# Expert outputs of the first layer written by scatter in token order and read back by plain loads

## The chip, the cores and the metric

One core of a Trainium2 chip runs the whole program in one launch. The core has a matrix engine (PE, with its weight loads as PEld), a vector engine (DVE), a scalar engine (ACT), a general engine (POOL) and a queue engine (SP). Each takes its instructions in order and waits on semaphores. Transfers between SBUF and DRAM run on 16 DMA engines and are issued from SP, ACT or POOL; such an issue stands in the engine's instruction order like any other. The metric is device time in microseconds (us) of one execution, lower is better.

## What is computed

A two-layer transformer over 256 image tokens and 256 context tokens, width 1024, all in 32 bits. Only the first layer updates the context, so its expert part works on 512 tokens (4 tiles of 128). What matters here is the expert part:

```python
def moe_ffn(h, ...):                       # h: tokens x 1024
    scores = sigmoid(t @ w_router)         # 16 experts in 4 groups of 4
    # best group, then its two best experts; their scores, normalised, are the gates
    for e in range(16):
        hid = silu(t @ w_gate[e]) * (t @ w_up[e])      # 1024 -> 256
        out = out + gates[:, e:e+1] * (hid @ w_down[e])  # 256 -> 1024
x = x + g2 * moe_ffn(...)                  # g2: a row of 1024, from the modulation
hx = rms_norm(x, norm1_g) * (1 + sc1) + sh1            # next layer's input
px = hx @ w_in                                          # next layer's projections
```

## The kernel before

Every product of the first layer runs as three 32-bit-reduced products (`mm3`): each operand is split into a high part (ACT casts, `whi`, `Xh`) and the rest (DVE subtracts, `wlo`, `Xl`).

**Experts of the first layer (`experts`, from L1006).** A token goes to two experts. For each of the 16 experts a list of at most 128 token numbers (`idx`) is made by the router. An indirect DMA from POOL gathers those rows of `h2row` (DRAM) into `xg` (L1025); PE transposes them, multiplies by gate and up (`first`), then by down (`second`, into two `y` banks of PSUM). ACT copies the banks to a `y` tile (L211; three such tiles take turns) and writes its 128 rows to `yrows` in DRAM from its own queue (`write`, L1095). So `yrows` is in order of expert and slot. The loop is software-pipelined: expert n's gate and up products stand beside the down products of expert n-1, and `write` comes one step later again. The second half of each w_down is split on POOL instead of DVE (L235 with engine POOL).

**From the first layer to the second (`next_in`, from L760).** `combine` fetches for each of the 4 token tiles the two rows of each token from `yrows` with two indirect DMAs on POOL (8 in all, L1393), by the row numbers `rows` that the router worked out. `sum_pairs` then has four steps a tile: `one` (ACT, L1405) scales the first by its gate, `both` (DVE, L1408) adds the second times its gate, `times` (L1411) multiplies by g2 (DVE for tile 0, POOL for tiles 1 to 3), `add` (DVE, L1414) adds to x. `tokens_in` normalises x: `square` (ACT, L226), `ms` (DVE, L219), `rstd` (a power on POOL, L221), `scale` (DVE `xn`, L655), `turn` (8 PE transposes, `tp`), `modulate` (`xf`, 4 columns blocks on ACT, 4 on DVE L684), `high` (ACT `Xh`), `low` (DVE `Xl`, L694). PE then runs 24 products of the first block of w_in for the tile. The order of these steps on each engine is written out by hand in `next_in`. The first w_in halves are split by four ACT casts and four DVE subtracts first (`parts`); the whi tiles of this stage lie where tiles of the expert stage lay, and so wait for their last readers.

**Waits.** The framework adds semaphore waits from overlaps of what instructions read and write. A scatter into a DRAM tensor counts as writing all of it.

Of the kernel before, what the change touches and what calls it, by code (L numbers as in the profile page):

```python
# [23 lines left out]
D = 1024  # L24
# [53 lines left out]
def shape_constants():  # L78
# [17 lines left out]
    k[:, C_GW:C_GW + 4] = np.array([4, 3, 2, 1], np.float32)  # L96
    k[:, C_TOK:C_TOK + 8] = np.tile(np.arange(4)[None, :] * 128 + i - NONE, 2)
    k[:, C_MH:C_EXP] = -0.5
# [76 lines left out]
class Model:  # L175
# [70 lines left out]
    def run(self, over):  # L246
        tc, nc, a = self.tc, self.nc, self.a
        self.over = over
        with ExitStack() as ctx:
# [8 lines left out]
            self.h2row = self.dram.tile([512, D], F32, name="h2row")  # L258
            self.yrows = self.dram.tile([NEXP * SLOTS * max(self.npass), D], F32, name="yrows")
            self.prow = self.dram.tile([PROWS, D], F32, name="prow")  # L260
# [264 lines left out]
    def layer(self, l):  # L525
# [51 lines left out]
        if paired:  # L577
            with self.psums(PS_PAIR):
                self.expert_pairs(l, mo, route)
        else:  # L580
            with self.psums(PS_MOE):
                self.experts(l, mo, route[0])
                self.gates, self.rows = route[1:]
        self.ring.close(mo)
# [175 lines left out]
    def next_in(self, l):  # L760

        ps = {}
        with self.tc.tile_pool(name="cb", bufs=1, side="right", reuse_waits="tile") as cb, self.tc.manual_schedule():
# [220 lines left out]
    def out_proj(self, l, work, mods):  # L984

        nc = self.nc
        route = Route(self, l, work, mods)
        fw = spread(FILL[l][2], 8)
        for cb in range(2):
            cs = slice(cb * 512, cb * 512 + 512)  # L990
            for t, ps in self.units("w_out", l, cb, [[t] for t in self.qtiles], self.mix_h, self.mix_l, self.q0,
                                    self.parts("w_out", l, cb)):
                if (t, cb) == (self.q0, 0):

                    route.modulation()
# [8 lines left out]
        return route.lists(), route.gates, route.rows  # L1004

    def experts(self, l, mo, lists):  # L1006
# [12 lines left out]
        def gather(n):  # L1019
# [3 lines left out]
            if n < 3:  # L1023
                nc.gpsimd.memset(xg[n], 0.0)
            nc.gpsimd.indirect_dma_start(  # L1025
                out=xg[n % 3], out_offset=None, in_=self.h2row[:, :],
                in_offset=bass.IndirectOffsetOnAxis(ap=lists[ps][:, e:e + 1], axis=0),
                bounds_check=T * 128 - 1, oob_is_err=False)
# [60 lines left out]
        def write(n):  # L1089
            ps, e = order[n]  # L1090
            y = mo.tile([128, D], F32, tag="y", name="y", bufs=3)
            for hf in range(2):
                self.copy(y[:, hf * 512:hf * 512 + 512], ys[n][hf], True)
            r0 = (e * self.npass[l] + ps) * SLOTS
            self.written = nc.scalar.dma_start(self.yrows[r0:r0 + SLOTS, :], y)  # L1095

        ring.until(l)
        with self.tc.manual_schedule():
# [6 lines left out]
            for n in range(N + 1):  # L1105
                if n:
                    turn(n - 1)
                if n > 1:
                    write(n - 2)
# [13 lines left out]
                if n == N - 1:  # L1123
                    ring.load(n=1)
            write(N - 1)

# [259 lines left out]
    def combine(self, l, cb):  # L1386

        self.pairs_of = {}
        n = NEXP * SLOTS * self.npass[l]
        for i, t in enumerate((0, 1, 2, 3) if l == 0 else (2, 3)):  # L1390
# [265 lines left out]
class Route:  # L1656


    def __init__(self, m, l, work, mods):
# [16 lines left out]
        self.gates = m.rt.tile([128, 2, T], F32, tag="gates", name="gates")  # L1676
        self.rows = m.rt.tile([128, 2, T], I32, tag="rows", name="rows")
        self.oh = tile_("oh", [2, T, 16])
        self.pos = tile_("pos", [2, T])
# [43 lines left out]
    def choose(self, x, i, r):  # L1723
# [92 lines left out]

        V.tensor_scalar(self.val[:, :, i], self.oh[:, :, i], cst[:, C_TOK + i:C_TOK + i + 1], None, OP.mult)
        self.picked(self.ips, i)
# [21 lines left out]
    def lists(self):  # L1840

        m, V, T = self.m, self.nc.vector, self.T
        lists, first = [], self.work.tile([128, 2, T], F32, name="first")
        for ps in range(m.npass[self.l]):
            ips = self.ips
            if ps == 0:
                V.tensor_copy(first, self.pos)
            else:
# [4 lines left out]
            idx = m.rt.tile([128, 16], I32, tag=f"idx{ps}", name="idx")  # L1853
# [5 lines left out]
        pick, e = self.small([2, T, 16], "picke"), self.small([2, T], "e")  # L1859
        V.tensor_tensor(pick, self.oh, self.k["cst"][:, C_EXP:C_EXP + 16].unsqueeze(1).unsqueeze(1).broadcast_to(  # L1860
            [128, 2, T, 16]), OP.mult)
        V.reduce_sum(e, pick, axis=AX.X)
        V.scalar_tensor_tensor(self.rows, e, float(SLOTS * m.npass[self.l]), first, OP.mult, OP.add)

# [42 lines left out]
    def extra(self):  # L1907
# [8 lines left out]
        V.tensor_scalar(eid, eid, 15.0, float(16 * self.l), OP.min, OP.add)  # L1916
        idf = small(1, "idf")
        V.scalar_tensor_tensor(idf, eid, 128.0, cst[:, C_ROW:C_ROW + 1], OP.mult, OP.add)
# [92 lines left out]
```

## Time and profile before

| | |
|---|---|
| time, median of 3 runs (lowest to highest) | 888.96 us (886.82 to 890.14) |
| the profiled execution's own time | 888.22 us |
| its span, first to last instruction | 886.3 us |
| PE busy over the span | 784.3 us (88%) |
| DVE, ACT, POOL busy | 582.4, 447.6, 222.2 us |
| experts of the first layer | about 336 to 501 us |
| first layer's experts to second layer's first products | about 500 to 546 us |

The span is that of one profiled execution; times on the trace count from its start. The profiled execution's time is 1.9 us above its span. Whatever delays PE at the border between the layers delays all that follows.

### The profile page before, as it was taken

What the parts mean: (1) busy time and instruction counts of PE and PEld (TensorE: products, weight loads), DVE (VectorE), ACT (ScalarE), POOL (GpSimd) and SP (SyncE); (2) the same over time, 40 slices, a digit from 0 to 9 for tenths busy, and PEclk for the clock granted to TensorE, in tenths of its full rate; (3) what the DMA queues carried; (4) which work ended last, traced back from release to release, by engine and by line L of the source; (5) the groups of instructions that cost most, each with busy time, mean ns of one, the idle gap of its engine ahead of it and who ended that gap; (6) DMA issues with size and microseconds to landing.
All of it is one profiled execution on the core that took longest, in us unless ns stands there. A gap on an engine that the chain in (4) does not pass through costs nothing.

```text
span 886.3 us, 12972 instructions
## 1 busy us (share of the span) xinstructions
PE 784.3 (88%) x4731; PEld 576.3 (65%) x4731; DVE 582.4 (66%) x1200; ACT 447.6 (50%) x861; POOL 222.2 (25%) x258
## 2 busy tenths in 40 slices
PE   4899999889989977999999549998899797999984
PEld 0578878445557746999999438887555565656541
DVE  1577673879863798899999586697667566221226
ACT  2454442667773416888888546462466543111112
POOL 2000101556320133443342472100423101000200
PEclk9999999999999988999999859999899997999987
DMA  9952221667879337899993757342188955999981
GB/s 319 344 185 96 95 96 48 247 270 284 275 214 376 121 148 263 306 388 401 400 408 156 249 195 292 128 158 95 51 331 215 340 186 215 350 423 422 419 333 51
DMA packets 54505, 219.18 MB, mean 247 GB/s; under 512 B 10299, under 2 KB 10299, under 8 KB 36640
## 3 DMA queue, kind: packets, MB, share of 16 engines
q1 hardware_dynamic: 40816, 182.34, 55.0%
q0 software_dynamic: 8736, 24.92, 7.9%
q10 hardware_dynamic: 4880, 11.00, 3.2%
q8 instruction: 39, 0.64, 0.3%
q14 instruction: 34, 0.28, 0.1%
HBM read 207.09 MB, written 16.84 MB: 253 GB/s over the span
## 4 chain that ended last, share of the span: by engine, by line
PE 66%; DVE 16%; DMA 8%; ACT 3%; issue 3%; POOL 2%; SPq 0%; ACTq 0%; POOLq 0%; DVEq 0%
PE mm L207 7%; PE mm L206 7%; PE mm L205 7%; PE tp L193 6%; PE gu L1189 6%; PE ada L459 4%; PE gu L207 4%; PE gu L205 3%; PE gu L206 3%; DMA wraw<-in_w_up 3%; PE sc L1466 3%; PE w L1245 3%; DVE wlo L235 2%; PE w L1154 2%; DVE nm L1480 2%
## 5 line engine op out<-in xcount | busy, mean ns | idle before, releaser
L235 DVE TENSOR_TENSOR wlo<-wraw,whi 128x1024 fp32r<-128x1024 f32 x136 | 186.1, 1392 | 43.0 <-ACT whi L234 40.5
L234 ACT CAST whi<-wraw 128x1024 fp32r<-128x1024 f32 x152 | 152.8, 1050 | 57.7 <-PE mm L207 35.5
L205 PE MATMUL mm<-whi,Xh 128*128 128x512 f32 x288 | 116.3, 405 | 5.1 <-ACT Xh L690 4.7
L206 PE MATMUL mm<-wlo,Xh 128*128 128x512 f32 x288 | 115.3, 400 | 0.5 <-DVE wlo L235 0.5
L207 PE MATMUL mm<-whi,Xl 128*128 128x512 f32 x288 | 115.0, 399 | 0.5 <-DVE Xl L694 0.5
L221 POOL TENSOR_TENSOR rstd<-ms,cst 128x1 f32<-128x1 f32 (+2 forms) x34 | 29.4, 864 | 272.1 <-DVE ms L219 263.2
L1493 ACT ACTIVATE e<-sc,nm 128x512 f32<-128x512 f32 (+1 forms) x96 | 58.4, 613 | 42.4 <-DVE nm L1486 22.6
L207 PE MATMUL gu<-whi,xl 128*128 128x256 f32 x256 | 74.3, 290 | 0.0
L205 PE MATMUL gu<-whi,xh 128*128 128x256 f32 x256 | 74.2, 290 | 0.0
L206 PE MATMUL gu<-wlo,xh 128*128 128x256 f32 x256 | 72.7, 284 | 0.0
L1189 PE MATMUL gu<-wraw,xq 128*64 128x256 f32 x512 | 64.4, 396 | 3.7 <-DMA wraw<-in_w_up 3.7
L205 PEld LDWEIGHTS mm<-whi,Xh 128*128 128x128 f32 x288 | 55.1, 191 | 18.7 <-ACT Xh L690 6.2
L207 PEld LDWEIGHTS mm<-whi,Xl 128*128 128x128 f32 x288 | 55.0, 191 | 13.9 <-DVE Xl L694 1.5
L206 PEld LDWEIGHTS mm<-wlo,Xh 128*128 128x128 f32 x288 | 55.1, 191 | 12.8 <-DVE wlo L235 1.2
L235 POOL TENSOR_TENSOR wlo<-wraw,whi 128x1024 fp32r<-128x1024 f32 x16 | 42.7, 2672 | 81.1 <-ACT whi L234 50.3
L1189 PEld LDWEIGHTS gu<-wraw,xq 128*64 128x64 f32 x512 | 37.9, 142 | 24.1 <-DMA wraw<-in_w_up 4.2
L193 PEld LDWEIGHTS tp<-ident,e 128*128 128x128 f32 x240 | 26.1, 142 | 40.8 <-issue 21.1
L1480 DVE TENSOR_REDUCE nm<-sc 128x1 f32<-128x512 f32 x64 | 41.2, 684 | 16.5 <-PE sc L1466 11.6
L207 PEld LDWEIGHTS gu<-whi,xl 128*128 128x128 f32 x256 | 49.3, 193 | 1.1 <-DVE xl L1050 0.4
L205 PEld LDWEIGHTS gu<-whi,xh 128*128 128x128 f32 x256 | 49.6, 194 | 0.3 <-ACT xh L1049 0.3
L206 PEld LDWEIGHTS gu<-wlo,xh 128*128 128x128 f32 x256 | 49.5, 193 | 0.0
L193 PE MATMUL tp<-ident,e 128*128 128x128 f32 x240 | 37.8, 286 | 8.4 <-DVE e L1534 3.9
(348 smaller groups left out, 1625.4 us busy)
## 6 DMA issues: line engine op xcount, KB each, us to landing
wraw<-in_w_ada SPq DMA_DIRECT2D x40, 1024.0 KB, 4.9
wraw<-in_w_gate SPq DMA_DIRECT2D x32, 1024.0 KB, 10.1
wraw<-in_w_up SPq DMA_DIRECT2D x32, 1024.0 KB, 11.0
wraw<-in_w_down SPq DMA_DIRECT2D x32, 1024.0 KB, 14.1
wraw<-in_w_in SPq DMA_DIRECT2D x14, 1024.0 KB, 5.2
wraw<-in_w_ada SPq DMA_DIRECT2D x16, 512.0 KB, 8.1
yrows<-y ACTq DMA_DIRECT2D x16, 512.0 KB, 8.1
wraw<-in_w_in POOLq DMA_DIRECT2D x5, 1024.0 KB, 11.9
```

The source lines that it names most:

```text
L193: self.nc.tensor.transpose(out, in_, self.k["ident"][:n, :n])
L205: mm(out, lhsT=xh, rhs=wh, start=start, stop=False)
L206: mm(out, lhsT=xh, rhs=wl, start=False, stop=False)
L207: mm(out, lhsT=xl, rhs=wh, start=False, stop=stop)
L221: nc.gpsimd.tensor_tensor(r, ms, self.k["mhalf"][:, :width], OP.pow)
L234: nc.scalar.copy(h, raw[:, lo:hi])
L235: (engine or nc.vector).tensor_tensor(l, raw[:, lo:hi], h.bitcast(F32), OP.subtract)
L459: nc.tensor.matmul(ps[32 * j:32 * j + 32, :], lhsT=self.silu_c[:, kc, :], rhs=raw[:, 512 * j:512 * j + 512], start=kc == 0, stop=kc == NKC ...
L1189: nc.tensor.matmul(gu[PSLOTS * g:PSLOTS * g + PSLOTS, 256 * b:256 * b + 256], lhsT=xq[q][:, kc, c:c + PSLOTS], rhs=raw[:, kc * 256:kc * 25 ...
L1245: nc.tensor.matmul(y[hf][gs], lhsT=hT[:, c, 0:PSLOTS] if p == NP else hT[:, c, gs], rhs=raw[:, c * D + o * 512:c * D + o * 512 + 512], sta ...
L1480: V.reduce_max(self.nm[:, i:i + 1], self.ps[i], axis=AX.X)
L1493: nc.scalar.activation(self.e[i][:, :self.nkey], self.ps[i], AF.Exp, scale=0.125, bias=self.nm[:, i:i + 1], accum_out=self.z[i])
```

## The change

Each expert's output rows are now scattered by an indirect DMA from POOL (new L1094) into `orow`, a DRAM tensor of 1024 rows in which token t's two results are rows 2t and 2t+1; empty slots get a row number out of bounds and are skipped. `combine` no longer gathers: for each tile two plain DMAs of 512 KB load the rows 2t (from SP's queue) and 2t+1 (from ACT's). The router makes one list `outs` of row numbers from the same one-hot product as before, and gets the token list `idx` from it by a shift; the old `rows` are not worked out any more. The g2 products of all four tiles run on DVE, and the hand-written order of `next_in` is changed. At the end of `experts`, the output of expert 14 is copied and written right after its products.

```diff
-    k[:, C_TOK:C_TOK + 8] = np.tile(np.arange(4)[None, :] * 128 + i - NONE, 2)
+    k[:, C_TOK:C_TOK + 8] = 2 * (np.arange(8)[None, :] // 2 * 128 + i) + np.arange(8)[None, :] % 2 - 2 * NONE
...
-            for name, t in (("one", 0), ("both", 0), ("times", 0), ("one", 1), ("add", 0)):
+            for name, t in (("one", 0), ("one", 1), ("both", 0), ("times", 0), ("add", 0)):
                 step(sums, t, name)
             step(ins, 0, "square")
             step(sums, 1, "both")
             step(ins, 0, "root")
-            step(sums, 1, "times", self.nc.gpsimd)
             step(sums, 2, "one")
             for t in range(1, 6):
                 step(ins, t - 1, "scale")
-                step(sums, t + 1, "both")
-                step(sums, t + 1, "times", self.nc.gpsimd)
-                step(sums, t, "add")
+                step(sums, t, "times")
                 for h in range(2):
                     step(ins, t - 1, "turn", h)
                     step(ins, t - 1, "modulate", h)
                 half(t - 2, 1)
                 step(ins, t - 1, "high", 0)
                 step(ins, t - 1, "high", 1)
+                step(sums, t, "add")
                 step(ins, t, "square")
                 step(sums, t + 2, "one")
                 step(ins, t - 1, "low", 0)
                 step(ins, t, "root")
+                step(ins, t - 1, "low", 1)
+                step(sums, t + 1, "both")
                 if t == 1:
                     self.ring.until(2, self.nc.gpsimd)
-                step(ins, t - 1, "low", 1)
                 half(t - 1, 0)
...
-            r0 = (e * self.npass[l] + ps) * SLOTS
-            self.written = nc.scalar.dma_start(self.yrows[r0:r0 + SLOTS, :], y)
+            self.written = nc.gpsimd.indirect_dma_start(
+                out=self.orow[:, :], out_offset=bass.IndirectOffsetOnAxis(ap=lists[ps][1][:, e:e + 1], axis=0),
+                in_=y, in_offset=None, bounds_check=2 * T * 128 - 1, oob_is_err=False)
...
-                if n > 1:
+                if 1 < n < N:
                     write(n - 2)
...
                 if n == N - 1:
                     ring.load(n=1)
+                    write(n - 1)
             write(N - 1)
...
-            y = [cb.tile([128, D], F32, tag="yc", name="yc", bufs=8) for _ in range(2)]
+            y = cb.tile([128, 2, D], F32, tag="yc", name="yc", bufs=4)
             for w in range(2):
-                self.nc.gpsimd.indirect_dma_start(
-                    out=y[w], out_offset=None, in_=self.yrows[:n, :],
-                    in_offset=bass.IndirectOffsetOnAxis(ap=self.rows[:, w, i:i + 1], axis=0),
-                    bounds_check=n - 1, oob_is_err=False)
-            self.pairs_of[t] = y, i
+                (self.nc.scalar if w else self.nc.sync).dma_start(y[:, w], rows[i, :, w])
+            self.pairs_of[t] = [y[:, w] for w in range(2)], i
...
-            V.tensor_scalar(idx, ips[:, 0:16], float(NONE), None, OP.add)
-            lists.append(idx)
+            V.tensor_scalar(out, ips[:, 0:16], 2.0 * NONE, None, OP.add)
+            V.tensor_single_scalar(idx, out, 1, OP.logical_shift_right)
+            lists.append((idx, out))
```

The scalar engine's order at the end of the expert loop and the start of `next_in` (the last row of casts splits the first w_in block) was before:

```order
L1067 ACTIVATE hid<-gu 128x256
L1077 CAST hh<-hT 128x256
L211 COPY y<-y 128x512 x2
L1095 DMA yrows<-y 128x1024
L211 COPY y<-y 128x512 x2
L1095 DMA yrows<-y 128x1024
L156 DMA wraw<-in_w_in 128x4x512
L234 CAST whi<-wraw 128x1024 x4
L1405 ACTIVATE yc<-yc,gates 128x1024 x2
```

and the same place on the same engine is now:

```order
L234 CAST whi<-wraw 128x1024 x3
L156 DMA wraw<-in_w_in 128x4x512
L234 CAST whi<-wraw 128x1024
L1067 ACTIVATE hid<-gu 128x256
L211 COPY y<-y 128x512 x2
L1077 CAST hh<-hT 128x256
L211 COPY y<-y 128x512 x2
L234 CAST whi<-wraw 128x1024 x4
L1396 DMA yc<-orow 128x1024 x4
L1405 ACTIVATE yc<-yc,gates 128x1024 x2
```

The writes have left this engine, the w_in load stands earlier, and the four loads of the second results stand behind the four casts. On POOL, from the split of the last w_down halves to the normalisation of the second layer's input, stood before:

```order
L235 TENSOR_TENSOR wlo<-wraw,whi 128x1024 x5
L1393 DMA yc<-yrows,rows 128x1024 x8
L221 TENSOR_TENSOR rstd<-ms,cst 128x1
L1411 TENSOR_TENSOR yc<-yc,wraw 128x1024 x2
L221 TENSOR_TENSOR rstd<-ms,cst 128x1
```

and now there stands, one scatter behind each split and the last two together:

```order
L235 TENSOR_TENSOR wlo<-wraw,whi 128x1024
L1094 DMA orow<-y,outs 1024x1024
L235 TENSOR_TENSOR wlo<-wraw,whi 128x1024 x2
L1094 DMA orow<-y,outs 1024x1024 x2
L221 TENSOR_TENSOR rstd<-ms,cst 128x1 x2
L156 DMA wraw<-in_w_in 128x4x512 x5
```

The eight gathers and the products are gone from POOL and sixteen scatters have come. In the built program each scatter waits for the landing of the scatter before it. On DVE the steps between one tile's scaling (`xn`) and the next tile's were before:

```order
L655 TENSOR_SCALAR xn<-xc,rstd 128x1024
L1408 SCALAR_TENSOR_TENSOR yc<-yc,gates 128x1024
L1414 TENSOR_TENSOR x_109<-x_109,yc 128x1024
L684 TENSOR_SCALAR xf<-tp,sc_2522,sh_2521 128x128 x4
L694 TENSOR_TENSOR Xl<-xf,Xh 128x4x128
L219 TENSOR_SCALAR ms<-nss 128x1
L694 TENSOR_TENSOR Xl<-xf,Xh 128x4x128
L655 TENSOR_SCALAR xn<-x_109,rstd 128x1024
```

and are now, for the same tile:

```order
L656 TENSOR_SCALAR xn<-xc,rstd 128x1024
L1411 TENSOR_TENSOR yc<-yc,wraw 128x1024
L685 TENSOR_SCALAR xf<-tp,sc_2522,sh_2521 128x128 x4
L1414 TENSOR_TENSOR x_109<-x_109,yc 128x1024
L695 TENSOR_TENSOR Xl<-xf,Xh 128x4x128
L219 TENSOR_SCALAR ms<-nss 128x1
L695 TENSOR_TENSOR Xl<-xf,Xh 128x4x128
L1408 SCALAR_TENSOR_TENSOR yc<-yc,gates 128x1024
L656 TENSOR_SCALAR xn<-x_109,rstd 128x1024
```

A product has come in, the sum to x has moved behind `xf`, and `both` of the tile after next has moved from the front to just ahead of the next `xn`.

## Rows read from the trace of the kernel before

**Rows 1.** Windows: length, PE, PEld, DVE, ACT, POOL busy (count), PEclk, DMA share, GB/s.

```profile
400.00:450.00 50.00, 50.00 (x363) 46.81 (x362) 47.71 (x47) 44.30 (x63) 21.08 (x10) 1.00 1.01 401
505.00:518.00 13.00, 0.00 (x0) 0.00 (x0) 10.19 (x10) 7.48 (x9) 10.34 (x10) 0.50 0.92 312
526.00:546.00 20.00, 20.00 (x89) 16.45 (x89) 13.22 (x25) 9.99 (x23) 9.22 (x9) 0.86 0.87 320
```

**Rows 2.** Timeline of PE, 518 to 546 us: the four tiles' transposes.

```profile
520.51 1.97 PE L193 MATMUL tp<-ident,xn 128*128 128x128 f32 x8 [20.12 <-DVE xn L655]
...
530.04 1.87 PE L193 MATMUL tp<-ident,xn 128*128 128x128 f32 x8
...
537.22 1.03 PE L193 MATMUL tp<-ident,xn 128*128 128x128 f32 x8
...
543.62 1.09 PE L193 MATMUL tp<-ident,xn 128*128 128x128 f32 x8
```

**Rows 3.** The chain that ended last, 500 to 504 us: start, us, what.

```profile
500.44 0.59 ACT y L211
501.05 2.96 DMA yrows<-y
```

**Rows 4.** Timeline of POOL, 490 to 518 us.

```profile
491.53 5.99 POOL L235 TENSOR_TENSOR wlo<-wraw,whi 128x1024 fp32r<-128x1024 f32 x2 [7.09 <-ACT whi L234]
504.95 1.00 POOL L1393 DMA_INDIRECT yc<-yrows,rows  x1 [7.43 <-DMA yrows<-y]
...
517.57 2.33 POOL L1411 TENSOR_TENSOR yc<-yc,wraw 128x1024 f32<-128x1024 f32 x1
```

**Rows 5.** Timeline of DVE, 511 to 535 us.

```profile
511.76 1.28 DVE L1408 SCALAR_TENSOR_TENSOR yc<-yc,gates 128x1024 f32<-128x1024 f32 x1 [0.79 <-DMA yc<-yrows,rows]
513.08 1.23 DVE L1411 TENSOR_TENSOR yc<-yc,wraw 128x1024 f32<-128x1024 f32 x1
514.34 1.23 DVE L1414 TENSOR_TENSOR xc<-xc,yc 128x1024 f32<-128x1024 f32 x1
...
516.78 0.15 DVE L219 TENSOR_SCALAR ms<-nss 128x1 f32<-128x1 f32 x1
517.62 2.83 DVE L655 TENSOR_SCALAR xn<-xc,rstd 128x1024 f32<-128x1024 f32 x1 [0.69 <-POOL rstd L221]
...
527.00 0.75 DVE L655 TENSOR_SCALAR xn<-xc,rstd 128x1024 f32<-128x1024 f32 x1 [0.45 <-POOL rstd L221]
...
531.95 1.37 DVE L684 TENSOR_SCALAR xf<-tp,sc,sh 128x128 f32<-128x128 f32 x4 [1.86 <-PE tp L193]
533.33 0.76 DVE L694 TENSOR_TENSOR Xl<-xf,Xh 128x512 fp32r<-128x512 f32 x1
```

**Rows 6.** Timeline of ACT, 490 to 512 us.

```profile
504.11 1.99 ACT L234 CAST whi<-wraw 128x1024 fp32r<-128x1024 f32 x2 [3.08 <-DMA yrows<-y]
```

**Rows 7.** The eight gathers into yc, issue to landing.

```profile
DMA to landing us min/median/max: 4.3/5.5/6.2
```

**Rows 8.** Timeline of POOL, 452 to 463 us, inside the expert loop.

```profile
452.58 2.65 POOL L235 TENSOR_TENSOR wlo<-wraw,whi 128x1024 fp32r<-128x1024 f32 x1 [5.13 <-issue]
455.61 1.57 POOL L1025 DMA_INDIRECT xg<-h2row,idx  x1 [0.39 <-ACT xh L1049]
462.33 2.63 POOL L235 TENSOR_TENSOR wlo<-wraw,whi 128x1024 fp32r<-128x1024 f32 x1 [5.15 <-ACT whi L234]
```

**Rows 9.** The gathers into xg, 395 to 450 us, issue to landing.

```profile
DMA to landing us min/median/max: 9.2/9.5/10.0
```

**Rows 10.** The writes of y, 395 to 450 us, issue to landing.

```profile
DMA to landing us min/median/max: 7.9/8.1/8.4
```

**Rows 11.** Timelines of DVE, POOL and PE at the router's end, 334 to 342 us.

```profile
334.74 0.17 DVE L1854 TENSOR_SCALAR idx<-ips 128x16 int32<-128x16 f32 x1
...
335.75 1.14 POOL L1025 DMA_INDIRECT xg<-h2row,idx  x1 [5.99 <-DVE gates L1867]
...
340.17 1.55 PE L193 MATMUL tp<-ident,xg 128*128 128x128 f32 x8 [2.00 <-DMA xg<-h2row,idx]
```

More of the change, by code (lines that the diff above doesn't have):

```diff
@@ L258, in run @@
             self.h2row = self.dram.tile([512, D], F32, name="h2row")
-            self.yrows = self.dram.tile([NEXP * SLOTS * max(self.npass), D], F32, name="yrows")
+            self.orow = self.dram.tile([1024, D], F32, name="orow")
             self.prow = self.dram.tile([PROWS, D], F32, name="prow")
@@ L582, in layer @@
                 self.experts(l, mo, route[0])
-                self.gates, self.rows = route[1:]
+                self.gates = route[1]
         self.ring.close(mo)
@@ L1003, in out_proj @@
             return route
-        return route.lists(), route.gates, route.rows
+        return route.lists(), route.gates
     def experts(self, l, mo, lists):
@@ L1026, in gather @@
                 out=xg[n % 3], out_offset=None, in_=self.h2row[:, :],
-                in_offset=bass.IndirectOffsetOnAxis(ap=lists[ps][:, e:e + 1], axis=0),
+                in_offset=bass.IndirectOffsetOnAxis(ap=lists[ps][0][:, e:e + 1], axis=0),
                 bounds_check=T * 128 - 1, oob_is_err=False)
@@ L1388, in combine @@
         self.pairs_of = {}
-        n = NEXP * SLOTS * self.npass[l]
-        for i, t in enumerate((0, 1, 2, 3) if l == 0 else (2, 3)):
-            y = [cb.tile([128, D], F32, tag="yc", name="yc", bufs=8) for _ in range(2)]
+        tiles = (0, 1, 2, 3) if l == 0 else (2, 3)
+        rows = self.orow[:, :].rearrange("(i p w) d -> i p w d", p=128, w=2)
+        for i, t in enumerate(tiles):
+            y = cb.tile([128, 2, D], F32, tag="yc", name="yc", bufs=4)
             for w in range(2):
-                self.nc.gpsimd.indirect_dma_start(
-                    out=y[w], out_offset=None, in_=self.yrows[:n, :],
-                    in_offset=bass.IndirectOffsetOnAxis(ap=self.rows[:, w, i:i + 1], axis=0),
-                    bounds_check=n - 1, oob_is_err=False)
-            self.pairs_of[t] = y, i
+                (self.nc.scalar if w else self.nc.sync).dma_start(y[:, w], rows[i, :, w])
+            self.pairs_of[t] = [y[:, w] for w in range(2)], i
     def sum_pairs(self, t):
@@ L1676, in __init__ @@
         self.gates = m.rt.tile([128, 2, T], F32, tag="gates", name="gates")
-        self.rows = m.rt.tile([128, 2, T], I32, tag="rows", name="rows")
-        self.oh = tile_("oh", [2, T, 16])
+        self.oh = tile_("oh", [2, T, 16], F16)
         self.pos = tile_("pos", [2, T])
@@ L1815, in choose @@
                                    accum_out=self.pos[:, w, i:i + 1])
-        V.tensor_scalar(self.val[:, :, i], self.oh[:, :, i], cst[:, C_TOK + i:C_TOK + i + 1], None, OP.mult)
+        V.tensor_tensor(self.val[:, :, i], self.oh[:, :, i], cst[:, C_TOK + 2 * i:C_TOK + 2 * i + 2].unsqueeze(2)
+                        .broadcast_to([128, 2, 16]), OP.mult)
         self.picked(self.ips, i)
@@ L1842, in lists @@
         m, V, T = self.m, self.nc.vector, self.T
-        lists, first = [], self.work.tile([128, 2, T], F32, name="first")
+        lists = []
         for ps in range(m.npass[self.l]):
             ips = self.ips
-            if ps == 0:
-                V.tensor_copy(first, self.pos)
-            else:
+            if ps:
                 V.tensor_scalar(self.pos, self.pos, -float(SLOTS), None, OP.add)
@@ L1852, in lists @@
                     self.picked(ips, i)
-            idx = m.rt.tile([128, 16], I32, tag=f"idx{ps}", name="idx")
-            V.tensor_scalar(idx, ips[:, 0:16], float(NONE), None, OP.add)
-            lists.append(idx)
+            idx, out = (m.rt.tile([128, 16], I32, tag=f"{n}{ps}", name=n) for n in ("idx", "outs"))
+            V.tensor_scalar(out, ips[:, 0:16], 2.0 * NONE, None, OP.add)
+            V.tensor_single_scalar(idx, out, 1, OP.logical_shift_right)
+            lists.append((idx, out))
         if m.over is not None:
             V.reduce_max(m.over[:, self.l:self.l + 1], self.pps[:, 64:80], axis=AX.X)
[L1859 to L1863, printed above, removed]
         pick, gsum, g = self.small([2, T, 16], "pickg"), self.small([T], "gsum"), self.gates
@@ L1916, in extra @@
         V.tensor_scalar(eid, eid, 15.0, float(16 * self.l), OP.min, OP.add)
-        idf = small(1, "idf")
+        idf = small(1, "px")
         V.scalar_tensor_tensor(idf, eid, 128.0, cst[:, C_ROW:C_ROW + 1], OP.mult, OP.add)
```

## The prediction

> **What bounds the kernel now.** I read the busy time by stretch first, since shares over the whole span mix stages. In the expert loop PE is busy for all of 50.00 us at full clock [rows 1]; a change of what surrounds it there costs or gives nothing until PE has to wait. At the border between the layers it is the other way round: from 505 to 518 us PE does nothing. So the second view is PE's timeline there [rows 2]: its first transposes start at 520.51 after 20.12 us of idle time that DVE's `xn` ended; the next three tiles' transposes follow at 530.04, 537.22 and 543.62 with PE busy all the way (20.00 of 20.00 us) [rows 1]. The first gap is at half the granted clock and PE keeps it for some 10 us after it starts again. What lies in the gap I take from the chain that ended last and the timelines of the other engines. The last y tile is copied by 501.03, its write lands 2.96 us after issue, at 504.0 [rows 3]; POOL's first gather starts at 504.95 [rows 4]; the second row of tile 0 has landed at 511.76, when DVE's `both` starts [rows 5]; from there it is a chain of `both`, `times`, `add`, square, root, `xn` to PE. Three things are to be seen. ACT's first w_in cast waited 3.08 us for the last write of y, since its tile takes the place of y [rows 6]. DVE's first `xn` took 2.83 us, the second 0.75 us: the first ran beside POOL's `times`, which began at 517.57 [rows 4, 5]. And eight gathers by POOL are what the tiles wait for, at 4.3 to 6.2 us from issue to landing [rows 7].
>
> **The expert loop: sixteen writes move from ACT to POOL.** ACT loses an issue per expert; PE is the bound there, so that gives nothing. POOL gets one indirect DMA per expert. The nearest row is its own gather there, 1.57 us; the scatter comes when the y copies are done, and POOL sits idle 5.15 us before its next `wlo` [rows 8]: the issue is hidden, 0. If that cover went, the second half of w_down would come late and PE would wait for it. One rule speaks against the move: the gather of 1.57 us ran beside DVE's subtracts, others without them took 1.0 us, as the first of [rows 4]. The Trainium skill (SBUF — State Buffer, Who interferes with whom) says that a DMA issued from POOL can be starved of descriptors by DVE and that one issued from ACT or SP cannot; the trace agrees with a stretch of 0.6 us and no more, which fits in the idle time, so that by row and rule alike the sum gets 0.
>
> The scatters carry a wait that the writes did not have: each waits for the landing of the one before. Behind the waiting one on POOL stand the next `wlo` and gather. In the loop a scatter is due every 9.75 us (462.33 - 452.58 [rows 8]); gathers land after 9.2 to 10.0 us there [rows 9], writes of y after 7.9 to 8.1 and 8.4 [rows 10]. I take 8 to 9, below the period, as the loop loses the ACT queue's 512 KB per expert and gets only the filled slots back: 0. The other end is a rival below.
>
> **The border, term by term.** POOL's last split ended at 497.5 [rows 4], and scatter 14 stands behind it. ACT's load of w_in needs the slot that POOL's split before reads, and now stands ahead of the cast for the last split: I let that make the split end some 0.3 later, and start scatter 14 at 498.0. Scatter 15 needs its copy (501.0) and the landing of scatter 14. No row shows a scatter in an idle stretch. Bounds: 2.96 us, the last plain write [rows 3], and 6.2 us, the slowest gather [rows 7]; I take 4.3 us, the fastest gather, which is issued by the same engine in the same way with empty queues. Then scatter 14 lands at 502.3, scatter 15 starts at 502.7 (0.4 us from a landing to the next issue, less than the 0.95 us of the gather that followed the write [rows 3, 4], as it waits for less) and lands at 507.0. The four casts, behind the same y tiles' release, take 4.0 us (1.99 for two [rows 6]) to 511.1, as w_in has long landed. Only behind them does ACT issue its loads: 511.4. A load of 512 KB lands after 2.96 us alone [rows 3] or 5.5 us amid the others [rows 7]; SP's four loads are still under way, so 4.0 us: tile 0 is complete at 515.4, against 511.76 before, +3.6 us.
>
> DVE's `xn` for tile 0 now runs without POOL's product beside it: 0.75 in place of 2.83 us, -2.1 us [rows 5].
>
> Then the tile loop. DVE's work between two `xn` is now 0.75 + 1.23 (`times`) + 1.37 (`xf`) + 1.23 (`add`) + two `Xl` of 0.76 + 0.15 (`ms`) + 1.28 (`both`) = 7.5 us [rows 5]. PE's period at full clock is 543.62 - 537.22 = 6.4 us [rows 2]. While PE is at half clock (530.04 - 520.51 = 9.5 us) DVE's 7.5 us are hidden; for the two periods after that they are not, 2 x 1.1 = +2.2 us. Lower bound +1.0 (DVE's instructions overlap by some 0.08 us each, eight of them, twice); upper bound +3.4, if `ms`, which stands ahead of the second `Xl`, also makes DVE wait 0.6 us for ACT's square, now that `add` comes later.
>
> At the router `idx` comes some 0.3 us later: `outs` takes its place, of 0.17 us, and a reduce stands between the two [rows 11]. POOL's first gather follows `idx`, and PE's first transposes waited 2.00 us for that gather [rows 11]: +0.3 us. `picke`, `e` and `rows` fall away behind it, hidden: 0. Putting expert 14's copies ahead of `hh` costs 0: the copies and `hh` both had to be done before the last products.
>
> Sum: 3.6 - 2.1 + 2.2 + 0.3 = +4.0 us. From 526 us PE runs without a gap [rows 1], so the delay goes through to the end. On the profiled execution's 888.22 us that is 892.2; the median of the runs is 0.7 higher, so I say 893.0 for the median.
>
> **Rivals.** What a measurement of this kernel can tell from no change is about 0.5%, 4.4 us: 884.5 to 893.4.
>
> *Writes that land fast.* If the scatters land in 2.96 us, as the last plain write did [rows 3]: scatter 14 at 501.0, scatter 15 from 501.4 to 504.4, casts to 508.4, ACT's loads at 508.7, tile 0 at 512.5 with the same 4.0 us, +0.7 - 2.1 + 2.2 + 0.3 = +1.1: 890. For it: a write needs no read of DRAM ahead. Against it: issue by POOL alone takes 1 us. The Trainium skill (DMA: Bandwidth & Descriptors, Anatomy of one DMA) puts a POOL-issued transfer at 2.0 us plus bytes at 436 GB/s, an estimate of 2.6 us for the half-filled 512 KB; by that the sum would be about 0.7 us lower than this rival's.
>
> *Slower: the chain of scatters falls behind in the loop.* They share POOL's software queue with the gathers, which land after 9.2 to 10.0 us [rows 9]. From a landing of 9.75 us on each scatter is later than the one before. At 10.3 us it is 0.56 us per expert over some 11 experts at full DMA load, 6 us; I let 2 us of that be hidden, half in POOL's idle time [rows 8] and half between a split and its products, and PE waits some 4 us: 897. The same sign has a landing of 6.2 us twice at the border: +3.8, 897 too.
>
> *Faster.* If the writes land fast and DVE's longer loop is hidden behind PE after all: 0.7 - 2.1 + 0.3 = -1.1, 888; less than 884.5 needs ACT's loads to land without the wait for the casts too, 4 us earlier. Nothing in the order of ACT lets that happen.
>
> **Chances.** Sum as worked out (892 to 894.5): 0.53, of which 0.31 under 893.4. Writes that land fast: 0.20. Late scatters: 0.23. Faster: 0.04. So faster 0.04, same 0.31 + 0.20 = 0.51, slower 0.22 + 0.23 = 0.45. The likeliest is 893.0, by itself 891 to 895. The range goes from 889 (the fast landing with the lower bound of the loop) to 898 (the late scatters).
>
> **What would show it.** The scatter of expert 15 starting some 0.4 us after the landing of that of expert 14; the first w_in cast near 507; ACT's yc loads issued near 511 and tile 0's `both` near 515.4; `xn` at 0.75 us; PE's first transposes near 522 and the third and fourth 7 to 8 us apart. In the loop PE stays at 100% and POOL's `wlo` starts as soon as ACT's cast is done. I am wrong if scatters land in under 3 us or over 6 us at the border, if PE has gaps in the loop, or if PE's transposes stay 6.4 us apart.

## The result and the profile after

The changed kernel took 896.18 us (median of 4 runs, 895.66 to 899.16) beside 888.8 us for the kernel before (4 runs, 886.82 to 890.14): a ratio of 1.0093, 95% interval 1.0066 to 1.0119. By the medians it is 7.4 us slower; the ratio stands for 8.3 us (5.9 to 10.6). The profiled execution took 899.16 us with a span of 897.3 us, 3 us above the median, so positions on its trace stand up to 3 us later than in a usual run. I compare distances between landmarks, not positions.

Windows of the profile after, with the columns of [rows 1]:

```profile
400.00:450.00 50.00, 49.46 (x357) 46.14 (x357) 49.76 (x46) 43.29 (x61) 28.36 (x16) 1.00 0.99 364
505.00:518.00 13.00, 0.88 (x4) 0.38 (x2) 5.59 (x5) 6.21 (x7) 0.96 (x1) 0.71 0.58 215
```

In the loop PE is still the bound, at 49.46 of 50 us, and DVE is now as full as PE (49.76). PE's one wait in this stretch is for DVE's `hid`:

```profile
414.53 0.50 PE L193 MATMUL hT<-ident,hid 128*128 128x128 f32 x2 [0.54 <-DVE hid L1068]
```

PE's timeline after, the counterparts of the last of [rows 11] and of [rows 2]:

```profile
343.98 1.94 PE L193 MATMUL tp<-ident,xg 128*128 128x128 f32 x8 [3.31 <-DMA xg<-h2row,idx]
...
523.72 1.97 PE L193 MATMUL tp<-ident,xn 128*128 128x128 f32 x8 [17.85 <-DVE xn L656]
533.32 1.50 PE L193 MATMUL tp<-ident,xn 128*128 128x128 f32 x8
541.25 1.09 PE L193 MATMUL tp<-ident,xn 128*128 128x128 f32 x8 [0.62 <-DVE xn L656]
548.10 1.09 PE L193 MATMUL tp<-ident,xn 128*128 128x128 f32 x8
```

PE's gap at the border got shorter, 17.85 us beside 20.12, and not longer as forecast. The four tiles are 9.6, 7.9 and 6.9 us apart beside 9.5, 7.2 and 6.4. But PE's wait for the first gather of the experts rose from 2.00 to 3.31 us. DVE's four subtracts of the first expert weights stood there in the kernel before:

```profile
336.47 4.63 DVE L235 TENSOR_TENSOR wlo<-wraw,whi 128x1024 fp32r<-128x1024 f32 x4
```

DVE and POOL after:

```profile
337.59 0.17 DVE L1853 TENSOR_SCALAR idx<-outs 128x16 int32<-128x16 int32 x1
...
338.51 4.63 DVE L235 TENSOR_TENSOR wlo<-wraw,whi 128x1024 fp32r<-128x1024 f32 x4 [0.23 <-ACT whi L234]
```

```profile
338.60 2.15 POOL L1025 DMA_INDIRECT xg<-h2row,idx  x1 [6.34 <-DVE gates L1863]
...
503.74 0.98 POOL L1094 DMA_INDIRECT orow<-y,outs  x1
507.69 0.96 POOL L1094 DMA_INDIRECT orow<-y,outs  x1 [2.98 <-issue]
```

POOL's first gather took 2.15 us to issue, with DVE's four subtracts beside it from its start. Before it took 1.14 us [rows 11], and the subtracts began 0.72 us after it (336.47 - 335.75). The two last rows are the scatters of experts 14 and 15 at the border. ACT, SP and DVE behind them:

```profile
505.23 1.27 ACT L211 COPY y<-y 128x512 f32<-128x512 f32 x2 [2.45 <-PE y L207]
511.04 1.04 ACT L234 CAST whi<-wraw 128x1024 fp32r<-128x1024 f32 x1 [4.54 <-DMA orow<-y,outs]
511.25 0.82 ACTq L1396 DMA_DIRECT2D yc<-orow  x2
```

```profile
510.97 2.06 SPq L1396 DMA_DIRECT2D yc<-orow  x4
```

```profile
512.12 4.63 DVE L235 TENSOR_TENSOR wlo<-wraw,whi 128x1024 fp32r<-128x1024 f32 x4 [8.88 <-ACT whi L234]
517.05 1.29 DVE L1408 SCALAR_TENSOR_TENSOR yc<-yc,gates 128x1024 f32<-128x1024 f32 x1 [0.30 <-DMA yc<-orow]
...
522.91 0.75 DVE L656 TENSOR_SCALAR xn<-xc,rstd 128x1024 f32<-128x1024 f32 x1 [0.69 <-POOL rstd L221]
```

The cast waited for the last scatter, whose `y` tile's place it takes. It began 3.35 us after the scatter's start (511.04 - 507.69); the landing itself stands in the trace 3.20 us after it, and that of expert 14's scatter 3.22. The loads into yc were issued while the first cast ran, not behind the fourth. Tile 0's `both` then stood behind DVE's four subtracts and waited 0.30 us more for its rows. From the last copy of y (506.50) to `both` it is 10.55 us; before it was 10.73 (501.03 to 511.76 [rows 3, 5]).

So the border accounts for little, and the loss had to be looked for in front of it and behind it.

### The profile page after: what moved, and what is told of

It reads as the page before. It is cut to its first block, busy times and chain, and to the rows that moved or that the text cites. A ratio compares the mean times of both kernels' runs of the same rounds, so it can differ in the third digit from the quotient of the medians.

```text
span 897.3 us, 12986 instructions
## 1 busy us (share of the span) xinstructions
PE 794.0 (88%) x4731; PEld 581.2 (65%) x4731; DVE 588.4 (66%) x1200; ACT 447.4 (50%) x861; POOL 225.1 (25%) x263
## 3 DMA queue, kind: packets, MB, share of 16 engines
q0 software_dynamic: 9888, 24.92, 7.7%
## 5 line engine op out<-in xcount | busy, mean ns | idle before, releaser
L235 DVE TENSOR_TENSOR wlo<-wraw,whi 128x1024 fp32r<-128x1024 f32 x136 | 191.5, 1437 | 39.2 <-ACT whi L234 36.8
L205 PE MATMUL mm<-whi,Xh 128*128 128x512 f32 x288 | 118.3, 412 | 5.1 <-ACT Xh L691 4.7
L207 PE MATMUL mm<-whi,Xl 128*128 128x512 f32 x288 | 117.0, 406 | 0.6 <-DVE Xl L695 0.6
```

Source lines behind the costliest of these rows:

```text
L205: mm(out, lhsT=xh, rhs=wh, start=start, stop=False)
L207: mm(out, lhsT=xl, rhs=wh, start=False, stop=stop)
L235: (engine or nc.vector).tensor_tensor(l, raw[:, lo:hi], h.bitcast(F32), OP.subtract)
```

## The experiments

All ratios are to the kernel before, run beside it on the same chip. The distances in the text come from one profiled execution of each kernel. Two readings ran through the series: that the sum of the prediction is right in its parts (border and DVE's loop), and that the traces show other causes.

**The first gather.** The removal of `picke`, `e` and `rows` was booked at nothing, since they are hidden. But they stood ahead of the four subtracts. The edit to the changed kernel:

```diff
+        pick, e, rows = self.small([2, T, 16], "picke"), self.small([2, T], "e"), self.small([2, T], "rows")
+        V.tensor_tensor(pick, self.oh, self.k["cst"][:, C_EXP:C_EXP + 16]..., OP.mult)
+        V.reduce_sum(e, pick, axis=AX.X)
+        V.scalar_tensor_tensor(rows, e, float(SLOTS), self.pos, OP.mult, OP.add)
```

> The changed kernel with three DVE operations of the router put back (picke, its sum e, and a product in place of rows; their result is not used). They stand between outs and the four subtracts of the first expert weights, so the subtracts start some 0.6 us later and the first gather of POOL is issued without them beside it. Theory A (the router cost 2.4 us because the subtracts run beside the gather's issue, 2.15 us in place of 1.14): the first gather takes 1.1 to 1.3 us on POOL again, PE's first transposes of xg start 1.0 us or more earlier against the router's own landmarks, and the time falls by 1 to 2 us against the changed kernel, to 894 to 895. Theory B (the router costs 0.3 us, for the later idx alone, as the sum on record has it): gather and time do not move, 896.

Measured: 892.49 us, ratio 1.0064 (1.0041 to 1.0088). By the ratios that is 2.6 us less than the changed kernel, more than the 1 to 2 us expected. The two intervals overlap, so the reading rests on the rows of POOL, DVE and PE in that run:

```profile
336.69 1.14 POOL L1025 DMA_INDIRECT xg<-h2row,idx  x1 [6.29 <-DVE gsum L1867]
```

```profile
337.28 4.63 DVE L235 TENSOR_TENSOR wlo<-wraw,whi 128x1024 fp32r<-128x1024 f32 x4 [0.30 <-ACT whi L234]
```

```profile
341.06 1.94 PE L193 MATMUL tp<-ident,xg 128*128 128x128 f32 x8 [1.43 <-DMA xg<-h2row,idx]
```

The gather is issued in 1.14 us again, since the subtracts start 0.59 us after it and not 0.09 us before, and PE waits 1.43 us for it in place of 3.31. Adding work to DVE gave time back. Theory A holds, B falls: with `idx` as late as in the changed kernel the gather is back at 1.14. The three added tiles also move some other tiles; the products of layer one's w_out, which they move, follow each other at 0.2330 us in place of 0.2334, under 0.1 us for all 192.

**Does a delay at the border go through?** On the kernel before, the first xn is written seven times over:

```diff
-                step(ins, t - 1, "scale")
+                for _ in range(7 if t == 1 else 1):
+                    step(ins, t - 1, "scale")
```

> The kernel before with the first xn of layer one's border written seven times over (six are dead work of 0.67 us each), so PE's first transposes come 4.0 us later and nothing else is changed. Theory C (what the sum on record took for granted: behind 526 us PE runs without a gap, so a delay goes straight through): +4.0 us, 892.5 to 893.5. Theory D (a shifted border moves where PE's clock falls to half in the attention of the second layer, as the two traces differ there by 3 to 5 us): the end moves by clearly more or less than the transposes, by 2 us or more, and the difference is found in matmuls of 0.63 us in place of 0.40 behind 600 us.

Measured: 892.45 us, ratio 1.005 (1.0033 to 1.0067), +4.4 us. The rows of the first and the last tile:

```profile
525.68 1.97 PE L193 MATMUL tp<-ident,xn 128*128 128x128 f32 x8 [24.92 <-DVE xn L655]
...
548.25 1.09 PE L193 MATMUL tp<-ident,xn 128*128 128x128 f32 x8
```

PE's idle time grew from 20.12 to 24.92, +4.8 (part of the dead work ran beside POOL's product); the tiles were 22.57 us from first to fourth in place of 23.11 [rows 2], and from the fourth to DVE's last operation it took 336.23 us beside 336.29. So 4.2 us went in at the border and 4.4 came out (2.9 to 5.9 by the interval): theory C holds, and theory D is not needed.

**DVE's order, alone and undone.** The order of the changed kernel with the gathers and writes of the kernel before, and the changed kernel with the old order. The core of the first (the second is its reverse):

```diff
-            step(sums, 1, "times", self.nc.gpsimd)
...
-                step(sums, t + 1, "both")
-                step(sums, t + 1, "times", self.nc.gpsimd)
-                step(sums, t, "add")
+                step(sums, t, "times")
...
+                step(sums, t, "add")
```

> The kernel before with the changed kernel's order of next_in alone: the g2 products of all four tiles on DVE, the gathers and the writes to yrows as before. The sum on record: xn beside no product of POOL, -2.1, the longer loop of DVE +2.2: the same time, 889, PE's tiles 7.5 us apart behind the second. By the trace of the changed kernel: -2.1 + 1.3 = -0.8, 888, tiles 9.5, 7.9 and 6.9 apart. A rival: the product of tile 0 and the order wait for gathers that land late, and nothing is gained, 890 or more.

> The changed kernel with the old order of next_in and the g2 products of tiles 1 to 3 on POOL again; lists, scatters and plain loads as changed. The sum on record: xn beside POOL's product again +2.1, shorter loop of DVE -2.2: the same time, 896. By the two traces +0.8: 897, with xn of tile 0 at 2.8 us and the tiles' transposes 9.5, 7.2 and 6.4 us apart. A rival: without the gathers POOL reaches its product earlier and is done before xn, so that xn stays at 0.75 us and the shorter loop is all that is left: 894.

Measured: the order alone 888.4 us, ratio 0.9999 (0.9982 to 1.0016); the old order in the changed kernel 897.09 us, 1.0109 (1.0088 to 1.013). Rows of DVE and PE of the first:

```profile
517.87 0.75 DVE L655 TENSOR_SCALAR xn<-xc,rstd 128x1024 f32<-128x1024 f32 x1 [0.69 <-POOL rstd L221]
```

```profile
518.68 1.97 PE L193 MATMUL tp<-ident,xn 128*128 128x128 f32 x8 [18.29 <-DVE xn L655]
528.27 1.60 PE L193 MATMUL tp<-ident,xn 128*128 128x128 f32 x8
536.29 1.09 PE L193 MATMUL tp<-ident,xn 128*128 128x128 f32 x8 [0.67 <-DVE xn L655]
543.14 1.10 PE L193 MATMUL tp<-ident,xn 128*128 128x128 f32 x8
```

and `xn` of the second:

```profile
525.68 2.84 DVE L656 TENSOR_SCALAR xn<-xc,rstd 128x1024 f32<-128x1024 f32 x1 [0.69 <-POOL rstd L221]
```

`xn` is 0.75 us wherever POOL's product is not beside it and 2.83 or 2.84 where it is. The first to the fourth tile takes 24.46 us with the new order and 22.55 with the old one in the changed kernel. The order gives 2.1 us and takes 1.4 to 1.9; its net cost is below what a run can tell. The rival that POOL would be done before `xn` without the gathers fell.

**The pitch of PE's products.** The changed kernel and the four of these experiments showed one more difference that no step of the prediction had: the 128x512 products of w_in and w_out follow each other at another pitch (the time from one start to the next). Kernels whose operands stand at the same addresses agree in it to 0.0009 us, others differ by up to 0.0055. In the built programs the changed lists take 32 bytes more per partition (`outs` 64 in place of `rows` 32), and the split weights of both w_in and of layer two's w_out, which are the moving operand, start 32 bytes lower. Those of layer one's w_out start 544 bytes higher, since tiles of the router have gone from the same pool. The test moves the split weights by an unused tile, the last one of the two pools. No instruction is added, but other tiles of these pools (`xn` and `xf` among them) move along:

```diff
+        self.wsp.tile([128, 8], F32, tag="pad", name="pad")
         close(in_cm)
...
+        work.tile([128, 8], F32, tag="pad", name="pad")
         close(wk_cm)
```

> The kernel before with an unused tile of 32 bytes per partition as the last one of the pools that hold the split weights of w_in and w_out, so these weights (the moving operand of the 128x512 products) start 32 bytes lower: at 96 or 32 bytes past a multiple of 128 in place of 0 or 64. Nothing is computed or moved otherwise. Theory L (the changed kernel's lists are 32 bytes larger, and where the moving operand no longer starts at a multiple of 64 bytes PE's products follow each other at 0.233 to 0.234 us in place of 0.228 to 0.230): the pitch of the products goes to 0.2341 before 200 us, 0.233 in 260 to 330 us and 0.233 in 530 to 600 us, and the time rises by 2.5 to 3.5 us (480 x 0.0008 + 192 x 0.0038 + 384 x 0.0054 = 3.2), to 890.5 to 891.5. Theory M (the slower pitch comes from the scatters, the loads or the chip's state): pitches and time as before, 888.

> The same with 64 bytes in place of 32: the weights move as far and further but start at multiples of 64 again. Theory L: pitches and time of the kernel before, 888. If any move of these tiles costs time: slower, as with 32 bytes or more.

> The changed kernel with the same unused 32 bytes, so the weights start at multiples of 64 again as in the kernel before. Theory L: pitches 0.2333, 0.230 and 0.228 as before, and 2.5 to 3.5 us less than the changed kernel, 893 (ratio 1.005 to 1.0065). Theory M: 896 still.

> The changed kernel with both: the three operations of the router put back, and the 32 bytes. If the two causes add up (gather and clock 2.5, pitch 3): 890 to 890.5, ratio 1.002 to 1.0035; what is left is the scatters' own cost in the loop and at the border, and the longer loop of DVE, less the faster xn. If they are one and the same cause: 892.5, no better than with the three operations alone.

Measured: kernel before with 32 bytes 892.05 us, 1.0059 (1.0036 to 1.0082); with 64 bytes 888.85, 1.0015 (0.9998 to 1.0032); changed kernel with 32 bytes 892.25, 1.0059 (1.0038 to 1.008); that with the three operations too 890.29, 1.0035 (1.0013 to 1.0057). Neighbouring products of w_out on PE's timeline, with 32 bytes:

```profile
273.04 0.40 PE L207 MATMUL mm<-whi,mixl 128*128 128x512 f32 x1
273.28 0.39 PE L205 MATMUL mm<-whi,mixh 128*128 128x512 f32 x1
273.51 0.40 PE L206 MATMUL mm<-wlo,mixh 128*128 128x512 f32 x1
273.74 0.39 PE L207 MATMUL mm<-whi,mixl 128*128 128x512 f32 x1
273.98 0.40 PE L205 MATMUL mm<-whi,mixh 128*128 128x512 f32 x1
```

and with 64 bytes:

```profile
272.23 0.39 PE L206 MATMUL mm<-wlo,mixh 128*128 128x512 f32 x1
272.46 0.39 PE L207 MATMUL mm<-whi,mixl 128*128 128x512 f32 x1
272.69 0.39 PE L205 MATMUL mm<-whi,mixh 128*128 128x512 f32 x1
272.91 0.39 PE L206 MATMUL mm<-wlo,mixh 128*128 128x512 f32 x1
273.14 0.39 PE L207 MATMUL mm<-whi,mixl 128*128 128x512 f32 x1
```

Four steps take 0.94 us in the one and 0.91 in the other. The mean distance of neighbouring starts, by stage (us; in brackets where the weights start, in bytes past a multiple of 128):

| | w_in, layer 1 | w_out, layer 1 | w_in, layer 2 | w_out, layer 2 |
|---|---|---|---|---|
| products | 480 | 192 | 384 | 96 |
| before | 0.2333 (0) | 0.2296 (0) | 0.2278 (64) | 0.2332 (32) |
| changed | 0.2341 (96) | 0.2334 (32) | 0.2332 (32) | 0.2312 (0) |
| before, 32 bytes | 0.2342 (96) | 0.2328 (96) | 0.2333 (32) | 0.2297 (0) |
| before, 64 bytes | 0.2327 (64) | 0.2283 (64) | 0.2333 (0) | 0.2333 (96) |
| changed, 32 bytes | 0.2325 (64) | 0.2298 (0) | 0.2333 (0) | 0.2332 (96) |

Every stage that starts at 32 or 96 runs at 0.2328 us or more. At 64 it is less, down to 0.2278; at 0 it is less for w_out, while w_in stays at 0.2333 in both layers, which the expectations for 64 bytes and for the changed kernel with 32 had wrong. From before to changed the pitch alone is worth 480 x 0.0008 + 192 x 0.0038 + 384 x 0.0054 - 96 x 0.0020 = 3.0 us. Theory M falls: unused bytes in the kernel before make its pitch that of the changed one.

The time moved by more than the pitch. That of the kernel before rose by 5.2 us with 32 bytes (3.2 to 7.3), more than the 2.8 us that its own pitches give; with 64 bytes it rose by 1.3 us (-0.2 to 2.8), where its pitches give 1.6. The changed kernel lost 3.0 us with 32 bytes, as theory L had it, but its own pitches give only 480 x 0.0016 + 192 x 0.0036 - 384 x 0.0001 - 96 x 0.0020 = 1.2 of that, since w_in of layer two stayed slow. What the pitch leaves over in these times is not explained; the tiles that moved along were not moved alone.

The two causes add up, as far as the intervals can tell. In ratios: changed 1.0093, with the three operations 1.0064, with the 32 bytes 1.0059, with both 1.0035. Each edit alone overlaps with the interval of the changed kernel (1.0066 to 1.0119); that of both together ends at 1.0057, below it. Of the 3.1 us that are left (1.2 to 5.1), w_in of layer two at 0.2333 in place of 0.2278 is 2.1.

**What is left, and better versions.**

> The changed kernel with the three operations of the router put back, and unused tiles sized so that the split weights start at 64 (both w_in stages), 64 (w_out of layer one) and 0 (layer two) bytes past a multiple of 128; in the run before with 32 bytes w_in of layer two stood at 0 and kept a pitch of 0.2333. If the start address of the moving operand alone sets the pitch, it comes to 0.2278 behind 530 us, 384 x 0.0055 = 2.1 us less than that run: ratio 1.0035 - 0.0024 = 1.001, 888.3. What is left of the change is then within 0.5% of the kernel before. If the pitch there has another cause it stays at 0.2333 and the ratio at 1.0035.

The edit is the padding in other sizes (96 bytes for w_in of layer two). Measured: 891.44 us, ratio 1.0032 (1.0009 to 1.0055). The pitch of w_in of layer two came to 0.2326 at 64, not to 0.2278 as in the kernel before at 64. Layer one's stages stood at 0.2326 and 0.2292. So the start address past a multiple of 128 isn't the whole rule.

The built programs show what that remainder hides. Past a multiple of 256 bytes, w_in of layer two starts at 64 in the kernel before and at 192 here. Sorted so, the four stages of all fourteen kernels fall in line:

| start past a multiple of 256 bytes | pitch, us |
|---|---|
| 64 | 0.2276 to 0.2297 |
| 128 | 0.2296 to 0.2314 |
| 192 | 0.2325 to 0.2327 |
| 0 | 0.2333 to 0.2334 |
| 32, 96, 160 | 0.2328 to 0.2336 |
| 224 | 0.2341 to 0.2342 |

In the table above, w_out at 0 past a multiple of 128 was at 128 past one of 256, and w_in at 0 was at 0. This is a fit to the runs at hand; no kernel was built to test it, and the changed kernel was never run with w_in of layer two at 64.

The next kernel has those sizes, the three operations of the router, the old order with `times` of tile 1 on DVE behind the first `xn`, and the last split of w_down on DVE:

```diff
-            w[u] = self.split(t, s * 1024, s * 1024 + 1024, nc.gpsimd if name == "w_down" and s else None)
+            w[u] = self.split(t, s * 1024, s * 1024 + 1024, nc.gpsimd if name == "w_down" and s and n < N - 1 else None)
...
+                if t == 1:
+                    step(sums, 1, "times")
```

> The same with the old order of next_in, but with the g2 product of tile 1 on DVE behind the first xn and those of tiles 2 and 3 on POOL, and with the last half of w_down split on DVE, which does nothing at the border, so that POOL issues the scatter of expert 14 before it. By the rows of the changed kernel: xn 0.75 us as there, the tiles 9.2, 7.2 and 6.5 us apart (1.5 us less for the three), scatter 14 some 1.2 us earlier and with it scatter 15 and tile 0 some 1 us: 2 to 2.5 us less than the run above, ratio 0.998 to 0.999. A rival: the split on DVE comes behind other work there and PE's last products wait for it, nothing is gained at the border.

Measured: 892.22 us, ratio 1.0043 (1.0016 to 1.0069): nothing gained. POOL's rows at its border:

```profile
497.30 0.97 POOL L1099 DMA_INDIRECT orow<-y,outs  x1 [3.03 <-ACT y L211]
502.31 0.97 POOL L1099 DMA_INDIRECT orow<-y,outs  x1 [4.03 <-ACT y L211]
```

and DVE's:

```profile
495.81 1.23 DVE L235 TENSOR_TENSOR wlo<-wraw,whi 128x1024 fp32r<-128x1024 f32 x1 [0.47 <-ACT whi L234]
496.96 0.41 DVE L1073 TENSOR_TENSOR hid<-hid,gu 128x256 f32<-128x256 f32 x1
...
506.73 4.63 DVE L235 TENSOR_TENSOR wlo<-wraw,whi 128x1024 fp32r<-128x1024 f32 x4 [7.93 <-ACT whi L234]
511.50 1.28 DVE L1413 SCALAR_TENSOR_TENSOR yc<-yc,gates 128x1024 f32<-128x1024 f32 x1
```

The last scatter now waits for its copy alone, and from the last copy (502.03) to `both` it is 9.47 us in place of 10.55. But the split stands ahead of `hid` on DVE, and from the last expert's transposes to that copy it takes 18.47 us in place of 17.63. That is the rival's mechanism, though the rows still leave 0.9 us of gain from those transposes to the fourth tile's (58.29 us, against 59.15 in the run above); the time, 1.0043 against 1.0032, shows none of it. And `both` now starts as soon as the four subtracts are done, without a wait for its rows.

Last, the same `times` edit on the kernel before, and that with the weights at 64, 64, 64 and 0:

> The kernel before with one edit: the g2 product of tile 1 on DVE behind the first xn in place of POOL ahead of it. xn 0.75 in place of 2.83 us; DVE's 1.23 us more fall into the stretch where PE runs at half clock. -2.1 us: 885 to 886, ratio 0.9975. A rival: DVE's product delays xf of tile 0 and the second tile, and half of it is given back: 0.999.

> The run above with the split weights at 64, 64, 64 and 0 bytes past a multiple of 128 in place of 0, 0, 64 and 32. By the pitches of the runs with moved tiles: 480 x 0.0007 + 192 x 0.0013 + 96 x 0.003 = 0.9 us less than the run above, ratio 0.9965. If addresses don't matter: no difference.

Measured: 888.15 us, 0.9995 (0.9978 to 1.0013), and 884.89 us, 0.9973 (0.9952 to 0.9993). `xn` fell to 0.75 us in the first, but its first two tiles are 10.14 us apart in place of 9.53, and of the other 1.6 us the time can't tell: its interval reaches from -2.0 to +1.2 us. The second is the fastest kernel of the series, 2.4 us below the kernel before by its ratio, with pitches of 0.2326, 0.2285, 0.2276 and 0.2299. Between the two only unused bytes differ; their intervals overlap, so the step of 0.0022 is likely and not certain.

## Why the prediction was right in its number and wrong in its parts

The time came out at 896.2, inside the range of 889 to 898, 3.2 us above the forecast of 893.0, and on the side of "slower by over 0.5%". The sum of +4.0 is not where the time went: its largest term, +3.6 at the border, measured +0.3, and the largest costs stood where it had +0.3 and nothing. That the time fell into the range is luck. By groups of profiled kernels (us):

| distance | with the old part | with the changed part | forecast | measured |
|---|---|---|---|---|
| router's mask products to the last expert's transposes | 148.0 to 149.2 (7 kernels) | 151.8 to 152.2 (3) | +0.3 | +3.3 |
| last copy of y to `both` of tile 0 | 10.6 to 11.2 (7) | 10.6 to 12.2 (6) | +3.6 | +0.3 |
| `both` to PE's first transposes of the border | 8.75 to 8.84 (4) | 6.67 to 6.68 (9) | -2.1 | -2.1 |
| first to fourth tile's transposes | 22.5 to 23.2 (5) | 23.4 to 24.6 (6) | +2.2 | +1.4 |

The measured column is the difference of the two groups' means. With the pitch (+3.0, of which up to 0.4 may stand in the last row too) it makes +5.9, against 7.4 by the medians and 8.3 by the ratio (5.9 to 10.6). What is missing stays open.

- *"At the router ... +0.3 us"* and *"`picke`, `e` and `rows` fall away behind it, hidden: 0"*: this step failed, and it is the largest miss. The operations were hidden, but they kept the subtracts away from the gather. With the three put back the first distance is 148.7 to 150.4 us (4 kernels), 2.2 us less by the means. The Trainium skill's rule that DVE can starve a DMA issued from POOL of descriptors (SBUF — State Buffer, Who interferes with whom) was weighed in the loop, where it costs nothing; this trace agrees with it at the router, 2.15 us beside 1.14, where PE waits for that gather. The same section has it that `tensor_tensor`, which the subtracts are, did not stall a DMA in a probe; here the issue beside them took 1.0 us more, and the measurement decides. PE's clock adds to it: behind the longer wait the first 256-column products take 0.41 us each for 4.1 us (345.79 to 349.88, granted clock 0.50), before for 2.4 us (341.58 to 343.96), and 0.28 after that. From the first to the last expert's transposes PE had half the clock (1.2 GHz) for 6.0 to 6.2 us in the three kernels with the changed part and for 0 to 3.7 in the seven with the old one. A longer wait is not the only thing that goes with it: two of the four kernels with the operations put back had 6.8 us of it behind a wait of 2.0, and in these two stands most of the 1 us that is left of the 3.3.
- *"Only behind them does ACT issue its loads: 511.4"*: failed. The loads stand behind the casts in ACT's order, but went out 0.21 us after the first cast began (511.25 and 511.04). And the scatters landed in 3.2 us, not 4.3. The terms of the border were 3.6; what ends last there is the landing of the last scatter, the cast, then DVE's four subtracts, 10.55 us in all, about as long as the write and the gathers took (10.73).
- *The scatters hidden in the loop*: right in the main. They land after 8.4 to 9.6 us between 395 and 450 us, under the period of 9.75, as the row says:

```profile
DMA to landing us min/median/max: 8.4/9.2/9.6
```

  Two of the sixteen scatters waited for the one before, 6.7 us in all, and no wait of PE is put down to them. But the prediction named gaps of PE in the loop as a sign of being wrong, and there is the one of 0.54 us for `hid`. That `hid` stood behind two subtracts of DVE that took 5.30 us (408.85 to 414.15), where the period before had 4.13, and POOL's own split ran beside them from 409.52, behind a scatter. That the scatter brought the split there is likely and not shown.

- *`xn` without POOL's product, -2.1*: right, in every kernel that has it. *DVE's longer loop, +2.2 (1.0 to 3.4)*: the mechanism was right and the size too large, 1.4. The sum put 7.5 us of DVE's work into both periods at full clock; the first of them came to 7.9 us with PE waiting 0.62 us for `xn`, but the second has no `both` of a further tile in it and came to 6.9.
- *"The delay goes through to the end"*: right, shown by the kernel with 4.2 us put in.
- Nothing in the prediction covers the pitch. It came from the tiles that the change resized and removed, 32 bytes in the lists for three of the four stages, and by its own sum it is the largest cost after the router.
- Neither rival with its price was it: the scatters didn't fall behind, and where they landed fast (3.2, close to the 2.96 of that rival), the time was not 890. At the border that rival came nearest, with +0.7 beside the measured +0.3; its own steps give +0.9, as 508.7 and 4.0 make 512.7 and not 512.5.

## What to carry to other kernels

Work that is hidden can still be of use where it stands: before an operation is taken out, look at what moves up beside a POOL-issued DMA that somebody waits for. After any change of tile sizes compare the start addresses of the operands (here past a multiple of 256 bytes) and the pitch of the same products in both traces, in stages that the change doesn't touch; a difference there is layout and not the idea that is being tried. And an order list tells what stands behind what, not that a DMA waits for the operations ahead of it to end.

## What was not expected of the hardware

The pitch of 128x512 products in 32 bits moved between 0.2276 and 0.2342 us with the start address of the moving operand; all stages with starts at odd multiples of 32 bytes were at 0.2328 or more, and past a multiple of 256 bytes the starts sort all of them. The expert products didn't follow it: at 96 (before) and at 64 (changed) the 256-column ones took 0.1199 us both, the 512-column ones 0.2307 and 0.2306. Why is open.

The length of a short wait alone does not decide PE's clock behind it. In layer two's projections, before the change:

```profile
604.14 0.41 PE L193 MATMUL tp<-ident,qBC 128*128 128x128 f32 x2 [2.46 <-DVE qBC L857]
604.63 0.40 PE L207 MATMUL mm<-whi,Xl 128*128 128x512 f32 x1
```

and at the same place after it:

```profile
609.26 0.58 PE L193 MATMUL tp<-ident,qBC 128*128 128x128 f32 x2 [2.15 <-DVE qBC L857]
609.49 0.77 PE L206 MATMUL mm<-wlo,Xh 128*128 128x512 f32 x1
610.06 0.63 PE L207 MATMUL mm<-whi,Xl 128*128 128x512 f32 x1
```

After an idle time of 2.15 us products took 0.63 us for some 3 us, at a granted clock of 0.52 (mean of 609.26 to 612.5 us); after one of 2.46 us they took 0.40, at 1.00. The scatter of the runs goes with the clock: over 35 runs of the kernel before on one chip, time and mean granted clock have a correlation of -0.82.
